# A hybrid encoder layer: the issue order of every engine comes from a list scheduler in the kernel

## The chip, the cores and the metric

The kernel runs on one core of one Trainium2 chip. The metric is device time in microseconds for one execution of the whole layer; three executions are taken and the median counts. Beside them stands one profiled execution, from which every duration in this document comes unless another is named.

## What is computed

One layer of a bidirectional encoder on x of 1024 tokens by 1024 features, all in float32:

```python
x = x + 0.5 * rmsnorm(swiglu(rmsnorm(x), w_gate, w_up, w_down))     # FFN1, 1024 -> 2816 -> 1024
h = rmsnorm(x); z = h @ w_in                                         # 1024 x 3456
y = concat(attention(z[:, :1536]), rwkv7(z[:, 1536:]))
x = x + rmsnorm(y @ w_out)
x = x + 0.5 * rmsnorm(swiglu(rmsnorm(x), ...))                       # FFN2
```

Attention has 8 heads of 64, rotary, with three dilated bands mixed by their softmax denominators. RWKV-7 has 8 heads and runs a delta-rule recurrence over the tokens in both directions:

```python
def _rwkv7_step(state, inp):
    r, w, k, v, kk, kka = inp
    sa = jnp.einsum('dbhvk,dbhk->dbhv', state, kk)
    state = state * w[..., None, :] - sa[..., :, None] * kka[..., None, :] + v[..., :, None] * k[..., None, :]
    y = jnp.einsum('dbhvk,dbhk->dbhv', state, r)
    return state, y
```

## The kernel before

Matrix products are done with each operand split into a rounded high part and a low rest (`split`, L186 on ScalarE and L187 on VectorE) and three matmuls (high x high, high x low, low x high). The stages follow one another in `run`:

- **FFN1**. `_GateUp` multiplies gate and up by a Strassen-like scheme with seven products for each of 22 column blocks j. A product (n, j) is twelve matmuls (L81) into one PSUM tile; `left` loads the weight block and, where needed, builds sums of blocks on VectorE (L60 to L63); `prepare` splits it; `gather` adds the product into rows on VectorE (L86) and applies SiLU on ScalarE (L94). `store` multiplies the halves (L114) and writes seven combinations of the hidden rows to DRAM from GpSimd's queue (L116). `down_sums` builds sums of w_down blocks on GpSimd (L145) and stores them. `down` then loads hidden rows and weight blocks again, splits them (g-tiles) and multiplies (L415).
- **Projection and attention**. `project_attention` and `project_rwkv` (L510) project columns of w_in; the streams r, k, v go to DRAM (`d_rk`, `d_v`, `d_vt`). `attention` runs eight heads through `far` and `near`.
- **Scan**. Tokens are taken in 16 chunks of 64, two to a block, both directions together. For block n, `prep` loads its streams (tile `in`), scales them (L810 to L822), forms products (L830, masked in L832) and stores triangular parts to DRAM; `solve` loads them back as X and inverts by 31 steps of two VectorE operations each (L866, L868), a copy (L870) ends it; `merge` loads the inverses and completes them; `chain` runs the recurrence chunk by chunk, with TensorE (L937, L941, L952), ScalarE (L944, L954, L970) and one state update on VectorE (L968). `prep` and `solve` run up to four blocks ahead of `chain`, in a few buffers. From block 3 on, `project_attended` multiplies attention's rows by their part of w_out in between (L1064, tile `po`), copies the result and stores it (L1084).
- **Finish, projection, FFN2**. `finish_half` normalizes and gates the scan's rows (tiles `f_...`, L995 and on), `out_project` multiplies them (L1064, tile `pw`), adds, normalizes and turns rows, then FFN2 runs as FFN1 does.

The order of work: the program's calls are traced in the order of the Python code. The framework's own scheduler then simulates the engines with its cost model and, for each engine, issues the first call in program order that is ready in the simulation. It also places the tiles in their buffers and sets the waits. In two places the kernel steers it: `high_priority` around the spreading of the first gain row, and `issue_after` around `down_sums`, which ties its GpSimd calls behind the store of the current hidden row. `reuse_waits="tile"` in `pool` makes a tile of a new pool wait only for those old tiles that lay in the same place. DMAs are issued from SyncE (`load`, most stores), GpSimd (`column`, hidden rows, streams, merges) and ScalarE; on each queue they leave in the order of that engine's list, and one that waits holds those behind it. Eight pairs of split weights (`WB`) and eight raw blocks (`RAW`) are buffered.

## Time and profile before

| | us |
|---|---|
| three executions | 2406.85, 2415.44, 2415.84 |
| median | 2415.44 |
| profiled execution, its own time | 2414.54 |
| span of its profile, first to last instruction | 2412.8 |
| HBM traffic, read and written, over the span | 257.53 MB, 125.89 MB |

In the views below, a row of a group gives line, engine, operation, tiles written and read, shape and count; then busy time and the mean of one in ns; then the engine's idle time just before such instructions, and what ended it. A row of a timeline gives the start, the duration and the same names; a q behind the engine's name is its sequencer, which waits and issues DMAs. A row of waits gives the total, the number and the longest. PEclk is the granted TensorE clock, 1.00 being full speed. PE stands for TensorE, DVE for VectorE, ACT for ScalarE, POOL for GpSimd, SP for SyncE. Matmuls are pipelined, so their busy times overlap and their mean is longer than the spacing.

### The profile page before, as it was taken

How to read it: one execution, taken by the hardware profiler on the slowest of the kernel's cores; microseconds unless marked ns; L12 is line 12 of the kernel's file. 1: busy time of each engine (PE TensorE's matmuls, PEld its weight loads, DVE VectorE, ACT ScalarE, POOL GpSimd, SP SyncE). 2: the span in 40 equal slices, each digit the busy share in tenths (PEclk: the TensorE clock that was granted, in tenths of full speed). 3: DMA queues.
4: the chain of work that ended last, by engine and by line, in shares of the span. 5: the costliest groups of instructions: out<-in, count | busy, mean ns of one | idle time of the engine just before them, and what ended most of it. 6: DMA issues, size and time to landing. Idle time of an engine off the chain costs nothing.

```text
span 2412.8 us, 39319 instructions
## 1 busy us (share of the span) xinstructions
PE 2244.5 (93%) x14532; PEld 1817.3 (75%) x14532; DVE 1774.7 (74%) x2949; ACT 1030.6 (43%) x1918; POOL 519.8 (22%) x636
## 2 busy tenths in 40 slices
PE   7999999999999998999987588878979999999997
PEld 5788888788786777787766577764768888887886
DVE  7999999855764446667565887416889999997565
ACT  5333323354675205666444455335542223335453
POOL 2344444300000010111101221103004543442000
PEclk9999999999999998999986597899989999999999
DMA  5344454676644315232376776438644444448655
GB/s 149 127 171 164 154 175 144 217 232 195 200 139 173 122 53 153 82 85 76 92 180 157 165 189 161 116 104 261 224 129 174 170 153 170 155 159 267 192 188 183
DMA packets 359763, 386.03 MB, mean 160 GB/s; under 512 B 73618, under 2 KB 268050, under 8 KB 359572
## 3 DMA queue, kind: packets, MB, share of 16 engines
q1 hardware_dynamic: 314272, 289.02, 39.6%
q0 software_dynamic: 27248, 86.05, 9.6%
q10 hardware_dynamic: 18052, 8.46, 1.3%
q8 instruction: 114, 1.87, 0.3%
q14 instruction: 77, 0.63, 0.1%
HBM read 257.53 MB, written 125.89 MB: 159 GB/s over the span
## 4 chain that ended last, share of the span: by engine, by line
PE 36%; DMA 6%; DVE 4%; ACT 2%; issue 2%; SPq 0%; POOL 0%; DVEq 0%; ACTq 0%; POOLq 0%
PE gu L81 17%; PE pd L415 9%; PE po L1064 2%; DMA in<-d_rk 1%; PE st L937 1%; PE pw L1064 1%; PE y L937 1%; PE lp L830 1%; DMA d_y<-yb 1%; DVE ttmp L866 1%; DVE Ti L868 1%; PE xu L941 1%; PE bp L838 0%; DMA f_y<-d_y 0%; PE pt L330 0%
## 5 line engine op out<-in xcount | busy, mean ns | idle before, releaser
L81 PE MATMUL gu<-xh,wh 128*128 128x512 f32 x704 | 277.9, 395 | 4.1 <-ACT wh L186 3.7
L187 DVE TENSOR_TENSOR wl<-raw,wh 128x512 fp32r<-128x512 f32 (+1 forms) x273 | 275.7, 1013 | 5.0 <-ACT wh L186 4.2
L81 PE MATMUL gu<-xl,wh 128*128 128x512 f32 x704 | 276.7, 393 | 0.0
L81 PE MATMUL gu<-xh,wl 128*128 128x512 f32 x704 | 276.3, 393 | 0.0
L186 ACT ACTIVATE wh<-raw 128x512 fp32r<-128x512 f32 (+1 forms) x273 | 167.8, 627 | 242.6 <-PE gu L81 96.9
L415 PE MATMUL pd<-gl,gwh 128*128 128x512 f32 x616 | 240.5, 390 | 2.5 <-DVE gl L187 2.5
L415 PE MATMUL pd<-gh,gwh 128*128 128x512 f32 x616 | 239.5, 390 | 0.6 <-DVE row L86 0.6
L415 PE MATMUL pd<-gh,gwl 128*128 128x512 f32 x616 | 239.7, 389 | 0.0
L86 DVE TENSOR_TENSOR row<-gu,row 128x512 f32<-128x512 f32 x308 | 206.7, 683 | 22.0 <-PE gu L81 21.0
L187 DVE TENSOR_TENSOR gwl<-graw,gwh 128x512 fp32r<-128x512 f32 (+1 forms) x176 | 118.1, 674 | 129.6 <-ACT gwh L186 127.6
L116 POOL DMA_DIRECT2D d_hid<-row x154 | 85.0, 553 | 562.3 <-DVE row L114 535.9
L186 ACT ACTIVATE gwh<-graw 128x512 fp32r<-128x512 f32 (+1 forms) x176 | 101.4, 576 | 192.7 <-PE pd L415 158.3
L81 PEld LDWEIGHTS gu<-xh,wh 128*128 128x128 f32 x704 | 133.9, 190 | 33.8 <-ACT wh L186 4.7
L81 PEld LDWEIGHTS gu<-xl,wh 128*128 128x128 f32 x704 | 133.7, 190 | 27.7
L81 PEld LDWEIGHTS gu<-xh,wl 128*128 128x128 f32 x704 | 133.5, 190 | 27.9 <-DVE wl L187 0.2
L415 PEld LDWEIGHTS pd<-gl,gwh 128*128 128x128 f32 x616 | 115.6, 188 | 28.1 <-DVE gl L187 4.2
L415 PEld LDWEIGHTS pd<-gh,gwh 128*128 128x128 f32 x616 | 115.5, 188 | 25.2 <-DVE row L86 1.0
L415 PEld LDWEIGHTS pd<-gh,gwl 128*128 128x128 f32 x616 | 115.7, 188 | 23.9
L187 DVE TENSOR_TENSOR gl<-raw,gh 128x512 fp32r<-128x512 f32 x160 | 112.4, 714 | 16.4 <-ACT gh L186 16.1
L94 ACT ACTIVATE row<-row 128x512 f32<-128x512 f32 x44 | 27.8, 632 | 220.5 <-DVE row L86 212.9
L145 POOL TENSOR_TENSOR ws<-ws 128x512 f32<-128x512 f32 x88 | 115.1, 1307 | 1.1
L186 ACT ACTIVATE gh<-raw 128x512 fp32r<-128x512 f32 x160 | 98.0, 621 | 29.2 <-DMA raw<-in_ffn_w_down_dram 21.6
(354 smaller groups left out, 5321.8 us busy)
## 6 DMA issues: line engine op xcount, KB each, us to landing
d_hid<-row POOLq DMA_DIRECT2D x154, 256.0 KB, 2.4
graw<-d_hid SPq DMA_DIRECT2D x132, 256.0 KB, 3.0
raw<-in_ffn_w_gate_dram SPq DMA_DIRECT2D x88, 256.0 KB, 3.1
raw<-in_ffn_w_up_dram SPq DMA_DIRECT2D x88, 256.0 KB, 3.6
ws<-in_ffn_w_down_dram SPq DMA_DIRECT2D x88, 256.0 KB, 4.5
d_ws<-ws POOLq DMA_DIRECT2D x88, 256.0 KB, 2.3
raw<-d_ws SPq DMA_DIRECT2D x88, 256.0 KB, 2.7
raw<-in_ffn_w_down_dram SPq DMA_DIRECT2D x66, 256.0 KB, 3.4
```

Of the source, the lines that this page charges most:

```text
L81: self.K.nc.tensor.matmul(ps, a[:, k, :], b[:, k, :], start=(k == 0 and i == 0), stop=(k == 3 and i == 2))
L86: add = lambda o, x: V.tensor_tensor(o, ps, x, op=OP.add)
L94: A.activation(y[:, 0], y[:, 0], AF.Silu)
L116: put = lambda n, y: G.dma_start(self.hid[n - 1, j // 2], y)
L145: G.tensor_tensor(o, a, b, op=OP.subtract)
L186: self.nc.scalar.activation(h, src, AF.Copy)
L187: (eng or self.nc.vector).tensor_tensor(l, src, h, op=OP.subtract)
L415: T.matmul(ps[x], a[:, ts], b, start=(m == 0 and k == 0), stop=(m == NM - 1 and k == 2))
L830: T.matmul(ps[par][:, pr, :], bk[hs, pr, i, ko:ko + 128], pt[hs, pr, i, :], start=True, stop=True)
L866: V.tensor_tensor(tv, X[:, s, s + 1:][:, :, None].to_broadcast([128, r, m]), Ti[:, s, 0:m][:, None, :].to_broadcast([128, r, m]), op=OP.mult)
L937: add = lambda o, a, b, start, stop: T.matmul(o, a, b, start=start, stop=stop, skip_group_check=True)
L1064: self.nc.tensor.matmul(ps, a[:, k, ts], w, start=(k == 0 and j == 0), stop=(k == 3 and j == 2))
```

## The change

`self.nc` becomes a `_Tape`. Its five engine attributes are recorders: a call such as `nc.vector.tensor_tensor(...)` is noted with its operands and does nothing yet. Pools are wrapped (`_Pool`), so that the tape knows which tile lies in which pool, tag and buffer and where each pool lies in memory. After `run` has recorded everything, `order` computes an order and `play` makes the calls, each tied to the one before it on its engine by an edge that asks for no wait. `wire` finds what each call must come after: calls that touch overlapping parts of a tile or of DRAM, the earlier users of a tile's buffer, and, for a pool that lies where a closed pool lay, all users of that old pool. `cost` gives each call a duration (`took`), a latency to others (`late`), a table-load flag (`load`) and, for a DMA, a time on a wire that all DMAs share (`moved`). `rate` gives each call the length of the longest path from it to the end. `order` walks simulated time: on each engine, among the calls that are ready when the engine is free, the one with the longest path goes first.

The diff, cut to its core (`_Pool` and `mask` only keep accounts of places and of overlapping parts, and are left out):

```diff
+LOADS = {AF.Exp: 1, AF.Sqrt: 2, AF.Silu: 3, AF.Tanh: 4}
...
+    def note(self, eng, method, args, kwargs):
...
+        op.after = [h for h in self.hold if h.eng == eng]
+        self.ops.append(op)
+        return op
+
+    def after(self, op):
+        self.hold = [op] if op else []
...
+    def wire(self):
...
+        for pool in self.pools:
...
+            for q in self.pools:
+                if q.space == pool.space and q.closed is not None and q.closed < pool.opened:
+                    if pool.at < q.at + q.size and q.at < pool.at + pool.size:
+                        q.done = q.done or gate(q.users)
+                        froms[q.done] = 1
+            if froms:
+                g = gate(froms)
+                for op in pool.users:
+                    given[op][g] = 1
+            for _, bufs, tiles in pool.tags.values():
+                for k, name in enumerate(tiles):
+                    if k >= bufs and name in users:
+                        g = gate(dict(users.get(tiles[k - bufs], {})))
...
+    def cost(self, op):
...
+        if op.method == "dma_start":
+            op.took, op.late = (560 if op.eng == "gpsimd" else 360), 1500
+            runs = [math.prod(q[1] for q in a.ap) // (a.ap[-1][1] if a.ap[-1][0] == 1 else 1) for a in (x, *op.ins)]
+            size = math.prod(q[1] for q in x.ap) * 4
+            op.moved = max(size / 320, max(runs) * 1.5)
+        elif op.eng == "tensor":
+            k, m = (op.args[1] if len(op.args) > 1 else x).ap[0][1], x.ap[0][1]
+            if op.method == "transpose":
+                op.took = 112 if k > 64 else 80
+            elif op.args[1].dtype == F32R:
+                op.took = max(64, 0.443 * n)
+            else:
+                op.took = 0.4 * n + 20 if m <= 64 else 0.8 * n + 8
+            op.late = 170
+        elif op.eng == "vector":
+            rate = 1.04
...
+            op.took, op.late = 150 + rate * n + (83 if "accum_out" in op.kwargs else 0), 35
+        elif op.eng == "scalar":
...
+            op.took = 165 + 0.87 * n + 95 * aps + (188 if "accum_out" in op.kwargs else 0)
+            op.load, op.late = LOADS.get(func, 0), 40
+        else:
+            op.took, op.late = (250 + 2.1 * n if op.method != "memset" else 130 + 0.8 * n), 40
+
+    def rate(self):
...
+            op.rank += op.took + op.late + op.moved
+            for p in op.preds:
+                same = p.eng == op.eng and p.method != "dma_start" if p.eng else False
+                p.rank = max(p.rank, op.rank - (p.late if same else 0))
...
+    def order(self):
...
+            t, e = best
+            while later[e] and later[e][0][0] <= t + 1e-6:
+                _, r, n, op = heapq.heappop(later[e])
+                heapq.heappush(heap[e], (r, n, op))
+            _, _, op = heapq.heappop(heap[e])
+            if op.load and op.load != loaded:
+                t, loaded = t + 1283, op.load
+            op.start = t
+            own = free[e] = t + op.took
+            end = own + op.late
+            if op.moved:
+                wire = max(wire, own) + op.moved
+                end = wire + op.late
+            out.append(op)
+            settle(op, end, own)
...
+    def play(self, ops):
+
+        last = {}
+        info = mybir.DependencyInfo(mybir.DependencyClass.NoSync, mybir.DependencyReason.DATA)
+        for op in ops:
+            i = getattr(getattr(self.nc, op.eng), op.method)(*op.args, **op.kwargs).ins
+            if op.eng in last:
+                self.tc.add_manual_dep(i, last[op.eng].name, info, reason="order")
+            last[op.eng] = i
...
-                with self.K.tc.issue_after(self.begun.ins):
-                    self.down_sums(j // 2)
+                self.K.nc.after(self.begun)
+                self.down_sums(j // 2)
+                self.K.nc.after(None)
...
-        self.nc = tc.nc
+        self.nc = _Tape(tc)
...
-        make_identity(nc, self.ident)
+        make_identity(self.tc.nc, self.ident)
...
-                with self.tc.high_priority():
-                    gain = self.spread_row(hand, ring, pt, "ffn1_pre_g")
+                gain = self.spread_row(hand, ring, pt, "ffn1_pre_g")
...
-        _Kernel(tc, io, out).run()
+        k = _Kernel(tc, io, out)
+        k.run()
+        k.nc.play(k.nc.order())
```

More of the change, by code (lines that the diff above doesn't have):

```diff
@@ L1 @@
+import heapq
 import math
@@ L33, in _ap, with __init__, tile, close @@
     return bass.AP(tensor=src.tensor, offset=src.offset + off, ap=pat)
+LOADS = {AF.Exp: 1, AF.Sqrt: 2, AF.Silu: 3, AF.Tanh: 4}
+class _Pool:
+    def __init__(self, tape, real, name, bufs, side, space):
+        self.tape, self.real, self.name, self.bufs, self.side, self.space = tape, real, name, bufs, side, space
+        self.tags, self.opened, self.closed = {}, tape.tick(), None
+        self.stack = tape.stacks.setdefault((space, side), [])
+        self.under = self.stack[-1] if self.stack else None
+        self.stack.append(self)
+        tape.pools.append(self)
+    def tile(self, shape, dtype, name=None, tag=None, bufs=None):
+        tag = tag or name
+        t = self.real.tile(shape, dtype, name=name, tag=tag, **({} if bufs is None else {"bufs": bufs}))
+        g = self.tags.setdefault(tag, [0, bufs or self.bufs, []])
+        size = math.prod(shape[1:]) * 4
+        g[0] = max(g[0], -(-size // 2048) * 2048 if self.space == PSUM else -(-size // 32) * 32)
+        g[2].append(t.tensor.name)
+        self.tape.home[t.tensor.name] = (self, tag, len(g[2]) - 1)
+        return t
+    def close(self):
+        assert self.stack.pop() is self
+        self.closed = self.tape.tick()
+    def place(self):
+        if not hasattr(self, "size"):
+            self.size = sum(size * n for size, n, _ in self.tags.values())
+            base = 0 if self.under is None else self.under.place()[1]
+            self.lo, self.hi = base, base + self.size
+            left, top = self.side == "left", 16384 if self.space == PSUM else self.tape.top
+            self.at = self.lo + (0 if self.space == PSUM else self.tape.base) if left else top - self.hi
+        return self.lo, self.hi
```

171 lines of the change are left out of this document (168 added, 3 removed).

## The prediction

> **What bounds the kernel now.** First the page: the span and the busy engines, then the same by stages, with idle time and TensorE's granted clock beside each other.
>
> ```profile
> span 2412.8 us, 39319 instructions
> ...
> PE 2244.5 (93%) x14532; PEld 1817.3 (75%) x14532; DVE 1774.7 (74%) x2949; ACT 1030.6 (43%) x1918; POOL 519.8 (22%) x636
> ```
>
> ```profile
> core 0: us, PE busy (x) PEld busy (x) DVE busy (x) ACT busy (x) POOL busy (x), PEclk, DMA share, GB/s
> 0.00:80.00 80.00, 61.47 (x262) 46.13 (x263) 63.94 (x106) 42.52 (x78) 12.18 (x24) 0.94 0.45 126
> 80.00:480.00 400.00, 397.98 (x1754) 328.54 (x1753) 382.88 (x418) 123.05 (x215) 179.97 (x209) 1.00 0.50 169
> 480.00:760.00 280.00, 278.35 (x1222) 222.56 (x1221) 181.63 (x265) 169.50 (x297) 3.79 (x7) 1.00 0.57 188
> 760.00:960.00 200.00, 186.90 (x1009) 143.14 (x1008) 87.78 (x162) 64.28 (x119) 14.79 (x21) 0.94 0.37 124
> 960.00:1200.00 240.00, 239.05 (x2201) 191.13 (x2200) 150.65 (x425) 139.12 (x304) 38.02 (x42) 0.97 0.29 83
> 1200.00:1640.00 440.00, 350.65 (x4879) 294.68 (x4877) 269.25 (x756) 192.37 (x356) 70.78 (x108) 0.79 0.60 155
> 1640.00:1800.00 160.00, 132.54 (x584) 97.73 (x584) 129.54 (x205) 81.50 (x158) 19.71 (x16) 0.91 0.62 204
> 1800.00:2160.00 360.00, 360.00 (x1590) 298.05 (x1589) 350.28 (x380) 108.65 (x190) 164.19 (x190) 1.00 0.48 164
> 2160.00:2400.00 240.00, 237.57 (x1044) 195.36 (x1043) 153.58 (x232) 107.79 (x197) 16.40 (x19) 1.00 0.64 207
> ```
>
> Two kinds of stage. In both FFNs (80 to 760 and 1800 to 2400) TensorE is busy 1273.90 of 1280 us at full clock: an order cannot shorten them, only spoil them. The slack is elsewhere: 18.5 us in the start, 13.1 in 760:960, 89.4 in the scan (1200:1640), 27.5 in 1640:1800. In the scan the clock is 0.79 as well, so its 350.65 us of matmuls are not all work at full speed. In attention (960:1200) TensorE has 0.95 us of idle time.
>
> So the scan decides. Which engine does it wait for? VectorE's groups there:
>
> ```profile
> L868 DVE TENSOR_TENSOR Ti<-Ti,ttmp 128x126 f32<-128x126 f32 (+22 forms) x248 | 61.3, 253 | 5.2
> L866 DVE TENSOR_TENSOR ttmp<-X,Ti 128x126 f32<-128x126 f32 (+22 forms) x248 | 61.1, 252 | 9.9 <-DMA X<-d_x 5.0
> L832 DVE TENSOR_TENSOR lm<-lp,k_tri 128x512 f32<-128x512 f32 x64 | 42.9, 686 | 15.9 <-PE lp L830 15.8
> L968 DVE TENSOR_TENSOR sv<-st,gc 64x512 f32<-64x512 f32 x24 | 16.5, 688 | 15.7 <-PE st L937 15.2
> L810 DVE TENSOR_TENSOR pr<-in,e 128x512 f32<-128x512 f32 x16 | 11.0, 689 | 26.2 <-DMA in<-d_rk 25.0 <-PE y L937 1.1
> ...
> L1055 DVE SCALAR_TENSOR_TENSOR wol<-wor,c_attn_out_g,woh 128x512 fp32r<-128x512 f32 x8 | 6.0, 747 | 2.0 <-ACT woh L1054 1.9
> ```
>
> Eight blocks pass through prep and solve on VectorE. Solve (L866, L868) is 122.4 us, prep is L832 with 42.9 and six 128x512 operations of about 11.0 each, of which L810 stands for all: 42.9 + 66.0 = 108.9. That is 231.3 us, 28.9 a block. The first and the last solve end with this copy, and the last chunk of the recurrence with that one:
>
> ```profile
> L870 DVE COPY X<-Ti x8: 587/594/733, 1262.9 to 1548.7; 128x512 f32<-128x512 f32 x8
> ```
>
> ```profile
> L970 ACT COPY yb<-y x32: 352/373/390, 1308.5 to 1618.8; 128x256 f32<-128x256 f32 x32
> ```
>
> From 1262.9 to 1548.7 are 285.8 us, in which VectorE owes seven blocks (7 x 28.9 = 202.3), the state updates (16.5), L1055 (6.0) and the copies of this row (8 x 0.59 = 4.7): 229.5. So up to 56 us of VectorE's time there go into waiting. After the last solve 70.1 us more pass to the last output copy. The end of the scan is this:
>
> ```profile
> 1548.66 0.61 DVE L870 COPY X<-Ti 128x512 f32<-128x512 f32 x1
> 1559.67 1.41 DVE L968 TENSOR_TENSOR sv<-st,gc 64x512 f32<-64x512 f32 x2 [10.40 <-PE st L937]
> ...
> 1575.23 0.68 DVE L968 TENSOR_TENSOR sv<-st,gc 64x512 f32<-64x512 f32 x1 [9.58 <-PE st L937]
> ...
> 1592.40 0.69 DVE L1072 TENSOR_TENSOR yat<-yat,rs 128x512 f32<-128x512 f32 x1 [15.16 <-DMA yat<-d_ya]
> ...
> 1594.35 1.41 DVE L968 TENSOR_TENSOR sv<-st,gc 64x512 f32<-64x512 f32 x2
> ```
>
> A state update every 15.6 us, then 19.1, then 24.5 to the last output copy: 59.1 us for three chunks. In the same stage the SyncE queue holds loads back:
>
> ```profile
> 1602.71 14.43 SPq L1084 DMA_DIRECT2D d_hp<-yao  x4
> 1618.55 0.33 SPq L182 DMA_DIRECT2D g2w<-in_rwkv_g_dram  x1
> 1618.93 1.64 SPq L182 DMA_DIRECT2D f_y<-d_y  x2
> ```
>
> Four stores of the attention half's projection sit ahead of the first loads of the finish stage, each waiting for its copy. The units that finish first need only blocks 2 to 5 of the scan, yet their loads leave after the last block.
>
> **The change part by part.** It adds no arithmetic, tile or DMA; 39319 instructions stay, but for waits and table loads. What moves is the order on five queues, SP's and POOL's DMAs among them, and each term is a wait that a better or worse order changes. Durations are of the profiled execution: 2414.54 us, of which the span is 2412.8; the median of the three runs is 2415.44.
>
> *Scan, middle.* The list takes the ready operation with the longest path behind it. Now prep(1) begins only when solve(0) has ended, and solve(1) 43.7 us after that (a 128x31 step is the first of a solve):
>
> ```profile
> 1262.90 0.59 DVE L870 COPY X<-Ti 128x512 f32<-128x512 f32 x1
> ...
> 1263.48 0.69 DVE L810 TENSOR_TENSOR pr<-in,e 128x512 f32<-128x512 f32 x1
> ...
> 1307.21 0.18 DVE L866 TENSOR_TENSOR ttmp<-X,Ti 128x31 f32<-128x31 f32 x1
> ```
>
> With the longest path first, block 1 goes ahead of blocks 2 and 3, since every later chunk hangs on it, and its loads go out ahead of theirs. Of the 56 us of waiting a part is the latency of store, load and merge between blocks, which no order removes. Ends: 0 and 56; I take somewhat under half, 25.
>
> *Scan, end.* If the state, value and output transfers are issued by landing time, and the projection's long matmuls only where the recurrence waits anyway, a chunk returns to the shorter steps. The shortest seen in these rows is 15.6; the state update itself is 0.69 us, so the rest is a chain of PE, ACT and VectorE that can be shorter when less lies between. Ends: 0, and the whole waiting of VectorE in the rows, 10.40 + 9.58 + 15.16 = 35.1. I take 20, above half, since two of these waits are for L937's matmuls and one for a load, and both stand in queues behind the projection's work.
>
> *Finish stage.* If its first units run beside the last two blocks, what is late next is the second half, which needs the last block. The stage's first wait on TensorE and the row above give the size: 14.43 us of queue, and the wait below of 10.2. Ends 0 and 24.6; I take 15.
>
> ```profile
> PE pt L330 <- DVE xl L187: 14.8, 9, 3.2
> PE lp L830 <- DVE Ti L868: 14.0, 1, 14.0
> ...
> PE yc L995 <- POOL f_y L994: 10.2, 2, 9.2
> ```
>
> *760:960 and 1640:1800.* 13.1 and 27.5 us of idle time, mostly chains of one tile (14.8 us behind L187 is such a chain, in several places). I take a fifth of both, 8; ends 0 and 40.6.
>
> *Start.* 18.5 us idle, waiting for x, then for normalization: same loads, same chain, so I take 0; ends 18.5 to either side, since a load put ahead of x costs what one put behind it gains. Dropping the high priority of the gain row costs nothing: its path to the first product is the longest there is.
>
> *Pool boundaries.* The recorder lets every user of a new pool wait, in its own arithmetic, for every user of the old pool beneath. The program itself waits tile by tile. So loads and splits of a following stage are listed behind the last operations of the previous one, at each FFN's step from gate/up to down first: there a rounding on ACT (below) and its split on VectorE (692 ns, next part), 1.3 us, now hide under matmuls, with the load before them. Two such places and the step into FFN2 at twice that each: minus 8. Ends: 0, and three times as much, as the stages between have such steps too.
>
> ```profile
> L186 ACT ACTIVATE gwh<-graw 128x512 fp32r<-128x512 f32 (+1 forms) x176 | 101.4, 576 | 192.7 <-PE pd L415 158.3
> ```
>
> *FFN interior.* Here VectorE is busy 350.28 of 360 us. Its parts:
>
> ```profile
> L187 DVE TENSOR_TENSOR wl<-raw,wh 128x512 fp32r<-128x512 f32 x114 | 124.4, 1091 | 0.4
> L86 DVE TENSOR_TENSOR row<-gu,row 128x512 f32<-128x512 f32 x135 | 90.5, 682 | 4.5 <-PE gu L81 4.2
> ```
>
> ```profile
> L187 DVE TENSOR_TENSOR gwl<-graw,gwh 128x512 fp32r<-128x512 f32 x54 | 37.4, 692 | 52.7 <-ACT gwh L186 52.6
> ```
>
> The list prices a 512-element VectorE operation at 150 + 1.04 x 512 = 682 ns. That fits L86 and the down stage's split (692), not the gate/up split, 1091 ns, in stages where POOL is busy 46% of the time (164.19 of 360 us; 3.79 of 280 in the down stage). The list thus believes in slack that isn't there. But eight rounded halves are buffered ahead of TensorE and the total work is the same, so I take 0; the price if that cover fails is the rival below. [...]
>
> *ACT tables.* The list charges a table load but does not choose so as to avoid one.
>
> ```profile
> L589 ACT ACT_TABLE_LOAD x4 | 5.1, 1283 | 0.1
> L691 ACT ACT_TABLE_LOAD x4 | 5.1, 1283 | 0.2
> ```
>
> Twice as many of these eight is 10.3 us of ACT, in a stage where ACT is busy 139.12 of 240 us: covered, 0; 10 if the cover is gone.
>
> Sum: 25 + 20 + 15 + 8 + 0 - 8 + 0 = 60 us. 2414.5 - 60 = 2354.5; I say 2354.
>
> **The rivals.** *More is recovered.* The upper ends of the scan and finish terms, 56 + 35.1 + 24.6 = 116, and 8 elsewhere without the boundary cost: 124, so 2414.5 - 124 = 2291. [...] Against: latencies of store, load and merge are inside those waits.
>
> *VectorE starves TensorE in gate/up (slower).* 2 FFNs x 22 column blocks x 7 products = 308 products. TensorE spends 3 x 4 matmuls on each; VectorE has 360 - 350.28 = 9.7 us of slack in 360, or 2.7%. If the order, arranged for splits of 682 ns, makes VectorE wait for TensorE once a product, it cannot make that up. Above 60 / 308 = 0.19 us lost a product the whole change is slower. At the mispricing itself, 0.41 us, it costs 126; at 0.3 us 92, so 2354.5 + 92 = 2447. For it: the two rows above. Against: the eight buffers, and L86 that waits 4.2 us in 135 now.
>
> *Nothing much moves.* The waits are those of the data: solve after load after store, chunk after chunk, two block buffers. Then the scan keeps its end and gains and boundary costs nearly cancel: 8 + 8 - 8 = 8, so 2406. An order that the program doesn't follow would give the same; but each instruction is tied to the one before it on its engine.
>
> **How the numbers follow.** Forecast 0.54, more recovered 0.17, starved 0.16, nothing 0.13. A measurement of this kernel can tell about 0.5%, 12 us, from no change. Faster by more: 0.54 + 0.17 = 0.71; within: 0.13; slower: 0.16. The range runs from 2290, the case that recovers more, to 2430, which takes in no change and mild starvation; left out are most of the starved case (0.11) and what may lie beyond the other (0.07): 0.18. The faster cases alone would be 2290 to 2400.
>
> **What would show it.** Right: scan stage shorter by about 45 us between the first and last L870 and from there to the last L970, solve(1) sooner than 43.7 us after solve(0), f_y loads before the last d_y stores, clock above 0.79, FFN stages with the same length to 5 us. Wrong: L81 waiting for L187 in the FFNs (the starved case); the last L870 as far behind the first as now; the finish loads still behind the recurrence's end.

## The result: slower by 4.5%, and the profile after

| | before | after |
|---|---|---|
| median of four executions (before: the three above and one more), us | 2411.14 | 2516.52 |
| span of the profile, us | 2412.8 | 2515.8 |
| granted clock, mean | 0.944 | 0.929 |

The ratio is 1.0447, 95% interval 1.0406 to 1.0488. The forecast was 2354, the range ended at 2430: wrong in sign. All calls of the new kernel are made from one line of `play` (L335), so its rows are told apart by their tiles. The top of its page:

```profile
span 2515.8 us, 39279 instructions
...
PE 2298.2 (91%) x14532; PEld 1857.3 (74%) x14532; DVE 1637.5 (65%) x2949; ACT 1046.2 (42%) x1918; POOL 537.2 (21%) x636
```

The same number of matmuls takes TensorE 54 us more, while VectorE has 137 us less to show: its work did not shrink, single operations became shorter (below). To see where, both profiles are cut at the same events, not at the same times: end of gate/up, end of down, the first matmul of the r, k, v projection (tile `zr`), the end of attention's last head (`ya`), the first `pr` of prep(0), the last `yb` of the scan, the last output product (`pw`), and the end of the second gate/up. Before:

```profile
core 0: us, PE busy (x) PEld busy (x) DVE busy (x) ACT busy (x) POOL busy (x), PEclk, DMA share, GB/s
0.00:465.90 465.90, 447.05 (x1962) 365.04 (x1963) 435.34 (x510) 160.03 (x284) 185.50 (x225) 0.99 0.48 157
465.90:683.80 217.90, 215.52 (x958) 176.19 (x957) 142.83 (x227) 118.42 (x219) 6.65 (x8) 1.00 0.68 220
683.80:921.50 237.70, 224.27 (x964) 168.72 (x962) 112.36 (x141) 98.86 (x154) 18.58 (x28) 0.97 0.34 122
921.50:1163.20 241.70, 240.11 (x2399) 191.11 (x2399) 163.24 (x480) 148.58 (x334) 30.66 (x30) 0.95 0.30 83
1163.20:1200.20 37.00, 37.00 (x163) 30.63 (x164) 13.13 (x19) 12.57 (x25) 7.36 (x13) 1.00 0.39 124
1200.20:1618.80 418.60, 338.12 (x4828) 285.99 (x4826) 263.94 (x745) 185.94 (x345) 65.70 (x104) 0.79 0.59 150
1618.80:1740.00 121.20, 97.53 (x415) 68.46 (x416) 81.19 (x130) 59.78 (x120) 24.79 (x20) 0.93 0.76 245
1740.00:2186.40 446.40, 433.74 (x1925) 357.67 (x1924) 424.40 (x490) 146.09 (x257) 173.92 (x201) 0.98 0.47 161
```

After:

```profile
0.00:464.50 464.50, 445.38 (x1962) 363.33 (x1963) 355.83 (x506) 165.71 (x285) 194.40 (x225) 1.00 0.48 156
464.50:690.70 226.20, 218.73 (x957) 178.58 (x956) 141.85 (x229) 121.47 (x216) 7.17 (x8) 0.98 0.66 213
690.70:937.70 247.00, 222.21 (x1052) 176.83 (x1050) 117.69 (x154) 101.05 (x164) 18.51 (x28) 0.92 0.34 122
937.70:1240.30 302.60, 293.11 (x2525) 231.22 (x2524) 183.14 (x490) 161.62 (x356) 36.02 (x34) 0.97 0.27 77
1240.30:1257.80 17.50, 16.32 (x81) 13.13 (x82) 5.65 (x8) 6.88 (x14) 4.79 (x10) 1.00 0.83 212
1257.80:1693.90 436.10, 340.35 (x4651) 280.45 (x4650) 262.01 (x738) 172.21 (x325) 64.10 (x102) 0.76 0.53 136
1693.90:1843.70 149.80, 115.71 (x458) 81.17 (x457) 86.72 (x132) 61.87 (x122) 23.75 (x20) 0.82 0.65 209
1843.70:2285.10 441.40, 433.36 (x1931) 357.15 (x1930) 345.16 (x484) 149.42 (x255) 181.63 (x201) 0.99 0.48 158
```

Stage by stage, in us: start with gate/up -1.4, down +8.3, the stage behind it +9.3, attention +60.9, from attention to prep(0) -19.5, scan +17.5, finish and output products +28.6, second gate/up -5.0, and the rest (226.4 against 230.7) +4.3. The sum is 103.0, the difference of the spans.

Three rows carry it. Attention, where TensorE was busy 240.11 of 241.70 us before, got more work and little more waiting (9.5 us of idle time instead of 1.6). What was added is the projection; these are its rows alone, before and after, in attention's window:

```profile
921.50:1163.20 241.70, 80.10 (x239) 43.92 (x239) 11.16 (x18) 0.95 0.30 83
```

```profile
937.70:1240.30 302.60, 134.22 (x438) 79.69 (x438) 21.34 (x36) 0.97 0.27 77
```

The columns are TensorE, its weight load and ScalarE. 199 matmuls, 66 of 176 groups of three, moved from behind attention into it. The scan, from which they went, should then have been shorter. It is longer: TensorE has 95.8 us of idle time in it instead of 80.5, at a clock of 0.76 instead of 0.79. Its marks of before have these counterparts:

```profile
L335 DVE COPY X<-Ti x8: 583/594/766, 1332.6 to 1630.4; 128x512 f32<-128x512 f32 x8
```

```profile
L335 ACT COPY yb<-y x32: 348/372/405, 1361.6 to 1693.9; 128x256 f32<-128x256 f32 x32
```

From the first solve's end to the last are 297.8 us (before 285.8), from there to the last output 63.5 (before 70.1). Where the prediction looked for 25 and 20 us, 12 were lost and 7 gained. Another 12 were lost ahead of both, from the first `pr` to the first solve's end (74.8 us, before 62.7), a stretch for which the prediction had no term.

At first the order did change as forecast. These are the ends of the second, fourth and fifth solve, before and after:

```profile
1345.26 0.59 DVE L870 COPY X<-Ti 128x512 f32<-128x512 f32 x1
1403.60 0.59 DVE L870 COPY X<-Ti 128x512 f32<-128x512 f32 x1
1436.03 0.73 DVE L870 COPY X<-Ti 128x512 f32<-128x512 f32 x1
```

```profile
1353.86 0.60 DVE L335 COPY X<-Ti 128x512 f32<-128x512 f32 x1
1409.58 0.60 DVE L335 COPY X<-Ti 128x512 f32<-128x512 f32 x1
1505.76 0.59 DVE L335 COPY X<-Ti 128x512 f32<-128x512 f32 x1
```

The second solve ends 21 us after the first instead of 82, the fourth 77 instead of 141. Then the fifth comes 96 us behind the fourth instead of 32, and the gain is gone.

### The profile page after: what moved, and what is told of

Read it like the earlier page. It is cut to its first block, busy times and chain, and to the rows that moved or that the text cites. A ratio compares the mean times of both kernels' runs of the same rounds, so it can differ in the third digit from the quotient of the medians.

```text
span 2515.8 us, 39279 instructions
## 1 busy us (share of the span) xinstructions
PE 2298.2 (91%) x14532; PEld 1857.3 (74%) x14532; DVE 1637.5 (65%) x2949; ACT 1046.2 (42%) x1918; POOL 537.2 (21%) x636
## 5 line engine op out<-in xcount | busy, mean ns | idle before, releaser
L335 ACT ACTIVATE wh<-raw 128x512 fp32r<-128x512 f32 (+1 forms) x273 | 167.1, 628 | 396.4 <-PE gu L335 253.6
L335 DVE TENSOR_TENSOR wl<-raw,wh 128x512 fp32r<-128x512 f32 (+1 forms) x273 | 221.5, 821 | 100.8 <-ACT wh L335 59.3
L335 PE MATMUL gu<-xh,wh 128*128 128x512 f32 x704 | 252.3, 393 | 6.7 <-DVE row L335 3.3
L335 DVE TENSOR_TENSOR row<-gu,row 128x512 f32<-128x512 f32 x308 | 204.8, 684 | 80.6 <-ACT wh L335 44.6
L335 PE MATMUL gu<-xl,wh 128*128 128x512 f32 x704 | 251.0, 391 | 0.0
L335 PE MATMUL gu<-xh,wl 128*128 128x512 f32 x704 | 246.1, 390 | 0.0
L335 POOL TENSOR_TENSOR row<-row 128x512 f32<-128x512 f32 x88 | 129.9, 1477 | 520.0 <-DVE row L335 392.7
L335 DVE TENSOR_TENSOR gwl<-graw,gwh 128x512 fp32r<-128x512 f32 (+1 forms) x176 | 110.5, 633 | 137.5 <-PE pd L335 108.3
L335 PE MATMUL pd<-gh,gwh 128*128 128x512 f32 x616 | 180.4, 395 | 13.3 <-DVE row L335 13.2
L335 PE MATMUL pd<-gl,gwh 128*128 128x512 f32 x616 | 180.1, 395 | 0.0
L335 PE MATMUL pd<-gh,gwl 128*128 128x512 f32 x616 | 179.7, 395 | 0.2 <-DVE gwl L335 0.2
L335 ACT ACTIVATE gwh<-graw 128x512 fp32r<-128x512 f32 (+1 forms) x176 | 100.7, 576 | 165.2 <-PE pd L335 139.1
L335 PEld LDWEIGHTS gu<-xh,wh 128*128 128x128 f32 x704 | 132.6, 188 | 38.5 <-DVE row L335 6.7
L335 PEld LDWEIGHTS gu<-xl,wh 128*128 128x128 f32 x704 | 132.6, 188 | 26.9
L335 PEld LDWEIGHTS gu<-xh,wl 128*128 128x128 f32 x704 | 132.0, 188 | 27.3 <-DVE wl L335 0.2
L335 PEld LDWEIGHTS pd<-gh,gwh 128*128 128x128 f32 x616 | 116.4, 190 | 39.0 <-DVE row L335 14.3
L335 PEld LDWEIGHTS pd<-gh,gwl 128*128 128x128 f32 x616 | 116.9, 190 | 25.2 <-DVE gwl L335 0.6
L335 PEld LDWEIGHTS pd<-gl,gwh 128*128 128x128 f32 x616 | 117.1, 190 | 24.8 <-issue 0.2
L335 PE MATMUL lp<-pr,bk 64*128 64x128 f32 x512 | 76.5, 379 | 48.6 <-DVE bk L335 25.6
L335 DVE TENSOR_TENSOR gl<-raw,gh 128x512 fp32r<-128x512 f32 x160 | 115.9, 730 | 6.7 <-ACT gh L335 6.4
L335 ACT ACTIVATE gh<-raw 128x512 fp32r<-128x512 f32 x160 | 99.4, 629 | 47.7 <-PE pd L335 36.7
L335 POOL TENSOR_TENSOR ws<-ws 128x512 f32<-128x512 f32 x88 | 117.7, 1338 | 3.0
```

The lines of the kernel that those rows point to most:

```text
L335: i = getattr(getattr(self.nc, op.eng), op.method)(*op.args, **op.kwargs).ins
```

## The experiments

The medians below are compared with the kernel before on the same chip; ratios are to it. The stages are those of the tables, "scan" always from the first `pr` to the last `yb`. Some expectations cut otherwise: where they give attention 320 us, it is counted from its own first product (in the kernel after from 920.2 to 1240.3), and a scan of 454 us is counted from attention's end. By the tables these two are 302.6 and, with the way to prep(0), 17.5 + 436.1.

### Four single causes

The first theory: the list wrongly took the projection into attention, where TensorE is full, by too low prices or by its ranks; the finish stage suffers from loads that stand behind others on SyncE. The rival: TensorE's work only moves.

**E1, the projection held.**

```diff
+            last = [o for o in nc.ops if o.eng == "tensor"][-1]
...
-            self.project_rwkv(zr, pz, x, [(4, 2), (6, 2), (1, 1), (2, 2)])
+            self.project_rwkv(zr, pz, x, [(4, 2), (6, 2), (1, 1)])
+            nc.after(last)
+            self.project_rwkv(zr, pz, x, [(2, 2)])
+            nc.after(None)
...
+            nc.after(last)
             self.project_rwkv(zr, pz, x, [(8, 2), (10, 2)])
+            nc.after(None)
```

> Edit: the kernel after, with the three blocks of the r, k, v projection that the kernel before computed after attention made to wait for attention's last TensorE operation. Theory A (the projection was moved out of the scan's idle TensorE time into attention, where TensorE is full): attention falls from 320 us to 250 to 270, the scan stays within 10 us of 454 since TensorE stands idle there, and the whole kernel takes 2440 to 2475 us. Rival (TensorE's work is only moved, the sum is conserved): what attention gives back the scan takes, and the time is within 12 us of 2516.

Measured: 2546.54 us, ratio 1.0583 (1.0547 to 1.0618). Attention fell to 263.4 us (by the expectation's cut to 280.9, where 250 to 270 was expected), but the way to prep(0) took 37.7 and the scan 482.7. The theory's first half holds in sign, its second falls: behind attention more was lost than it gave back, 20 and 47 us for 39. The rival, a conserved sum, is nearer, but the time is 30 us above its 2516.

**E2, dearer fp32 matmuls.**

```diff
-                op.took = 112 if k > 64 else 80
+                op.took = 112 if k > 64 else 180
...
-                op.took = 0.4 * n + 20 if m <= 64 else 0.8 * n + 8
+                op.took = max(106, 0.8 * n + 32 if m <= 64 else 1.6 * n + 20) if n < 8 else 0.8 * n + 32 if m <= 64 else 1.6 * n + 20
```

> Edit: the kernel after, with nothing changed but the list's prices of fp32 matmuls, about doubled to what the trace shows (a 64-column transposition 180 ns, small products at least 106 ns). Theory A by its first cause (the list packs too much into attention because it holds attention's own matmuls for cheap): fewer than 110 of the projection's groups of three matmuls stand in attention, against 146, and the time is 2440 to 2480 us. Rival (the order of ranks does it, whatever the prices): 140 or more groups stay there and the time is within 15 us of 2516.

Measured: 2599.12 us, ratio 1.0801 (1.0765 to 1.0837), the slowest of all, and outside both ranges. 145 groups stayed in attention. Too low prices of these matmuls are not why they went there. Nor do the traces show all the new prices: in the kernel after, busy time by count is 116 ns for the two-column products (`kn`, 7.4 us for 64; new price 106), but 96 for the 64-column transpositions (`bp`, 24.5 us for 256; 180) and 52 for the products with the values (`po`, 56.9 us for 1088; 83). The scan took 493.9 us, and its row is worth a look:

```profile
1286.50:1780.40 493.90, 437.11 (x4652) 333.02 (x4650) 264.44 (x738) 173.32 (x326) 64.42 (x102) 0.69 0.47 120
```

TensorE has 57 us of idle time, 39 less than in the kernel after, and as many matmuls take 97 us more, at a granted clock of 0.69.

**E3, program order as rank.**

```diff
-                        heapq.heappush(later[s.eng], (s.ready, -s.rank, s.n, s))
+                        heapq.heappush(later[s.eng], (s.ready, s.n, s.n, s))
...
-                    heapq.heappush(later[op.eng], (0.0, -op.rank, op.n, op))
+                    heapq.heappush(later[op.eng], (0.0, op.n, op.n, op))
```

> Edit: the kernel after, with the operations ranked by their place in the program instead of by the longest path behind them; prices and gates stay. Theory A by its second cause (the ranks put the projection ahead of late attention heads): attention falls to about 250 us and the time to 2420 to 2450 us, about the kernel before. If the prices or the whole-pool gates are at fault, the time stays above 2490 us.

Measured: 2585.15 us, ratio 1.0757 (1.0707 to 1.0806). 119 groups in attention, 277.2 us; scan 542.1. The framework issues by the same rule, first ready in program order, and takes 2407. So ranks explain a part of attention (146 against 119 groups) and none of the total. What is left between the two is whose simulated clock says which call is ready first, the list's, with its prices and its waits for whole pools, or the framework's; most of the 178 us must lie there.

**E4, the output weights by GpSimd.**

```diff
-            W = self.out_weights(self.pool(st, "wo"), 4)
+            W = self.out_weights(self.pool(st, "wo"), 4, queue=nc.gpsimd)
```

> Edit: the kernel after, with the eight loads of the time-mix output weights in the finish stage issued by GpSimd instead of SyncE. Theory C (these loads stand in SyncE's list behind the loads of the finish stage, which wait for the scan's end): the first lands before the finish products begin, the stage from the scan's last output to the last product falls from 150 us to about 130, and the time by 15 to 20 us to about 2498. Rival (the one raw buffer or the VectorE chain sets the stage): the stage stays within 5 us of 150 and the time within 8 us of 2516.

Measured: 2523.17 us, ratio 1.0481 (1.0444 to 1.0517); finish 148.8 us, as the rival had it. The first of these loads now leaves 36.2 us after the scan's last output instead of 43.8, and the stage is no shorter: the queue alone is not the cause.

### The recorder, the list and the binding taken apart

So the change has three parts that can be run alone: calls are recorded and made later, they are made in the list's order, and each is bound to the one before it on its engine. Theory D: the binding costs, since the list's clock is not the chip's. The binding's edges ask for no wait, and in every kernel here, the one before too, each engine's order is fixed when the program is built. "Not bound" means that the framework takes the recorded order as program order and lets its own simulated clock decide which ready call goes first. So what is called the cost of binding here is the order by the list's clock against the same priorities by the framework's.

**E6, not bound.**

```diff
-            if op.eng in last:
-                self.tc.add_manual_dep(i, last[op.eng].name, info, reason="order")
-            last[op.eng] = i
```

> Edit: the kernel after, with the calls made in the list's order but without the edges that tie each to the one before it on its engine, so that the framework's scheduler takes the list's order as program order and issues by its own clock. Theory D (the list's ranks are sound, and what costs is that each engine is bound to an order computed with a clock that the chip does not keep): most of the loss goes, 2410 to 2450 us. Rival R (the list's priorities are bad in themselves, whoever keeps the clock): within 20 us of 2516, or slower.

**E7, the recorder alone**, E6 and:

```diff
-        k.nc.play(k.nc.order())
+        k.nc.play(k.nc.ops)
```

> Edit: the kernel after, with the recorded calls made in the order in which the program made them and no edges: the recorder alone, without the list. If the recorder is neutral, and the framework's own scheduling is what the list replaced: 2400 to 2425 us, the kernel before. Rival (recording itself costs, since pools open and close without calls between and the ties of the weight sums are lost): 2440 us or more.

**E8, the list for the scan alone**, E7 with the part from the projection to the scan's end bound in the list's order; **E9, all but that part**, which is free in program order (E8's order is shown; E9's is its mirror):

```diff
...
-        k.nc.play(k.nc.order())
+        lo, hi = k.nc.part
+        k.nc.play(k.nc.ops[:lo] + [op for op in k.nc.order() if lo <= op.n < hi] + k.nc.ops[hi:])
```

> Edit: as the kernel with the recorder alone, but the operations from the r, k, v projection to the end of the scan are made in the list's order and tied to it; attention, the FFNs and the finish stage are left to the framework. My prediction (the list shortens the scan): 45 us gained, about 2366 us. Rival L (the scan is a loop of latencies through four block buffers, which no order shortens): 2395 to 2430 us. Rival H (the list's order harms the scan by itself, engines standing behind operations that come later than the list believed): 2430 us or more, with a scan from the first prep to the last output of over 430 us against 419 before.

> Edit: the complement: the operations from the r, k, v projection to the end of the scan are left to the framework in program order, all others are made in the list's order and tied to it. If the losses of the kernel after add up by stage: boundaries 7 and finish stage 29 us are kept, attention is no longer than before because the projection is free, so 2411 + 36 = about 2447 us. Rival (attention's own operations are slowed by the list's order even without the projection): attention's heads end 20 us or more after their place in the kernel before, and 2465 us or more.

Measured: E6 2524.86 us (1.0493, 1.044 to 1.0546), E7 2485.84 (1.032, 1.0278 to 1.0361), E8 2571.37 (1.0686, 1.0627 to 1.0746), E9 2454.81 (1.0201, 1.0154 to 1.0248). E7 was a surprise, and its stages say why: both gate/up stages are longer, 506.1 and 483.5 us against 465.9 and 446.4; the scan is 9 us shorter, the others are within 4.

```profile
0.00:506.10 506.10, 456.58 (x1961) 371.33 (x1962) 404.68 (x510) 166.52 (x284) 191.38 (x225) 0.96 0.44 145
1772.90:2256.40 483.50, 444.28 (x1924) 364.82 (x1923) 395.80 (x490) 150.50 (x257) 176.06 (x201) 0.95 0.44 148
```

Without the binding the ties of `down_sums` (`issue_after` before, `hold` after) are lost too, so E6, E7 and E8 carry that loss, and E6's total says nothing on theory D; its scan of 383.7 us does speak for it. E8's scan is 461.4 us, for rival H, and prep(0) begins only 87.0 us after attention's end, before 37.0. E9's attention is 262.6 us with 102 groups in it, finish and products 153.4: its time lies between the sum of the losses and the rival, its attention is the rival's.

**E10 and E11, the same with the ties put back**, in program order and in the list's order:

```diff
-            if op.eng in last:
-                self.tc.add_manual_dep(i, last[op.eng].name, info, reason="order")
-            last[op.eng] = i
+            for h in op.after:
+                self.tc.add_manual_dep(i, last[h].name, info, reason="tie")
+            last[op] = i
```

> Edit: the recorder alone, calls in program order, with the one thing that was lost in that kernel put back: the ties of the weight sums behind the store of the hidden row. If the 78 us that the recorder alone cost lie in those ties (both gate/up stages were 37 to 40 us longer there, all other stages within 5 us of the kernel before): both stages return to 444 to 448 us and the time to 2400 to 2420 us. Rival (something else in recording costs): 2440 us or more.

> Edit: the calls in the list's order with the ties of the weight sums, but not bound on any engine, so that the framework issues by its own clock. Its difference to the kernel after is then the binding alone. Theory D (the binding to the list's clock costs in the scan): the scan from the first prep to the last output is 384 us as in the unbound kernel without ties, against 436, attention stays at 300 to 320, and the time is 2440 to 2465 us. Rival (the unbound scan was short only because the FFNs had shifted everything): scan over 420 us and the time over 2490 us.

**E12**, E10 with only the scan's loop, first merge to last chain, in the list's order (`part` is the loop's first and last call):

```diff
...
-        k.nc.play(k.nc.ops)
+        lo, hi = k.nc.part
+        k.nc.play(k.nc.ops[:lo] + [op for op in k.nc.order() if lo <= op.n < hi] + k.nc.ops[hi:])
```

> Edit: program order with the ties, nothing bound; only the operations of the scan from the first merge to the last chain, the rest of attention's projection among them, are made in the list's order. Theory D with its second half (the list's priorities do shorten the scan, and the gain was paid away in attention): attention 242 us as in the kernel before, scan from the first prep to the last output 380 to 395 against 419, time 2370 to 2390 us, faster than both kernels. Rival L (the scan is a loop of latencies that no priority shortens): 2400 to 2420 us.

**E13**, the kernel after with only that loop not bound, its order kept:

```diff
-            if op.eng in last:
+            if op.eng in last and not self.part[0] <= op.n < self.part[1]:
                 self.tc.add_manual_dep(i, last[op.eng].name, info, reason="order")
-            last[op.eng] = i
+            if not self.part[0] <= op.n < self.part[1]:
+                last[op.eng] = i
...
```

> Edit: the kernel after, all of it in the list's order and bound to it, but for the operations from the first merge of the scan to its last chain, which keep the list's order and lose the binding. Theory D: attention stays at 320 us, the scan from the first prep to the last output falls from 436 to about 385, the time to 2460 to 2475 us. Rival (binding is harmless there): within 12 us of 2516.

| kernel | us | ratio (95%) | attention | scan | finish |
|---|---|---|---|---|---|
| E10 program order | 2418.45 | 1.0044 (1.0023 to 1.0066) | 240.0 | 416.7 | 123.3 |
| E12 list in the loop | 2419.61 | 1.0043 (1.0019 to 1.0067) | 239.3 | 403.5 | 131.3 |
| E11 list, not bound | 2451.01 | 1.0181 (1.0136 to 1.0227) | 303.4 | 393.9 | 143.8 |
| E13 after, loop not bound | 2460.26 | 1.0221 (1.0171 to 1.027) | 305.8 | 383.4 | 148.8 |
| after | 2516.52 | 1.0447 (1.0406 to 1.0488) | 302.6 | 436.1 | 149.8 |

The times of E11 and E13 lie in the ranges of theory D. The binding costs 65 us (E11 to after); lifted in the scan's loop alone it gives 56 back, the scan being 53 shorter (E13). Of these 53, 39 are idle time of TensorE and 14 its busy time:

```profile
1257.20:1640.60 383.40, 326.42 (x4648) 272.70 (x4647) 248.72 (x738) 173.71 (x326) 63.68 (x102) 0.78 0.59 155
```

The list's order by itself costs 33 (E10 to E11; in the two profiles 38): 63 in attention and 20 in the finish stage, against 20 that prep(0) comes closer to attention's end, 23 gained in the scan and smaller ones of both signs elsewhere. E12 misses its 2370 to 2390 us and falls into the range of rival L: the scan gains 13, less than expected, and 8 go back in the finish stage. Even the 13 are not clear of the spread between profiles, since the scan takes 410.0, 404.1 and 407.9 us in E7, E9 and E16 (below), all in program order. In E11, with 23, 178 matmuls fewer stand in the scan than in E10, since the projection went into attention; E12 keeps that as it was. In E12's profile attention also begins 10 us later than in E10, which the edit doesn't touch. So no net gain.

E3 and E10 make the same comparison for program order: the list's clock 2585.15 us, the framework's 2418.45. What is wrong in the list's clock stays open. Dearer matmuls (E2) made it worse; its waits for whole pools and its single wire for all DMAs were not changed.

The scan's parts, with the number of its matmuls; the last column but one is the recurrence itself, from the first `yb` to the last:

| us | first `pr` to first solve's end | to the last solve's end | to the last `yb` | first to last `yb` | matmuls |
|---|---|---|---|---|---|
| before | 62.7 | 285.8 | 70.1 | 310.3 | 4828 |
| after | 74.8 | 297.8 | 63.5 | 332.3 | 4651 |
| E10 program order | 61.4 | 282.6 | 72.7 | 307.9 | 4834 |
| E12 list in the loop | 63.0 | 290.0 | 50.5 | 302.6 | 4782 |
| E11 list, not bound | 76.1 | 264.8 | 53.0 | 288.0 | 4656 |
| E13 after, loop not bound | 74.1 | 256.3 | 53.0 | 277.3 | 4648 |

How one engine's order holds another is seen in the middle of the scan of the kernel after, ahead of the fifth block's solve (its first step is the last row here), in the 96 us that were lost. VectorE:

```profile
1456.41 0.69 DVE L335 SCALAR_TENSOR_TENSOR bk<-bk,th_w 128x512 f32<-128x512 f32 x1
1472.57 0.69 DVE L335 TENSOR_TENSOR th_a<-th_a,in 128x512 f32<-128x512 f32 x1 [15.48 <-ACT th_a L335]
1473.29 1.41 DVE L335 TENSOR_TENSOR sv<-st,gc 64x512 f32<-64x512 f32 x2
1474.73 0.19 DVE L335 TENSOR_TENSOR ttmp<-X,Ti 128x31 f32<-128x31 f32 x1
```

And ScalarE in the same time:

```profile
1465.80 0.58 ACT L335 COPY xs<-xu 128x512 f32<-128x512 f32 x1 [9.69 <-PE xu L335]
1466.28 1.19 ACT L335 ACTIVATE tt<-pb 32x512 f32<-32x512 f32 x2
...
1470.89 1.65 ACT L335 ACTIVATE th_a<-th_a,ka,kah 128x128 f32<-128x128 f32 x4
```

VectorE waits 15.48 us for four short activations of the next prep; they stand in ScalarE's list behind a copy of the recurrence, and this waits 9.69 us for TensorE. The state update and the fifth solve stand behind all of it. TensorE itself is not idle. The first row shows a product taken in one piece; from 1454.4 on three products of the recurrence are taken in turns of one to four matmuls, most of them two:

```profile
1440.93 1.15 PE L335 MATMUL xu<-sv,lm 128*64 128x64 f32 x30
...
1464.64 0.47 PE L335 MATMUL xu<-sv,lm 128*64 128x64 f32 x2
1465.04 0.31 PE L335 MATMUL pb<-tt,d 32*32 32x32 f32 x2
```

```profile
1456.00:1459.00 3.00, 3.00 (x34) 2.34 (x32) 1.09 (x2) 0.10 (x1) 0.00 (x0) 1.00 0.28 90
1459.00:1462.00 3.00, 3.00 (x26) 2.24 (x25) 0.00 (x0) 0.00 (x0) 0.00 (x0) 0.63 0.00 0
1462.00:1465.00 3.00, 3.00 (x22) 2.20 (x22) 0.00 (x0) 0.00 (x0) 0.00 (x0) 0.50 0.00 0
```

In one piece 30 matmuls of `xu` take 1.15 us. In turns 34 matmuls take 3.00 us at full clock, and then the granted clock falls to 0.50. So here the list's order of TensorE makes a delay, and the lists of ScalarE and VectorE pass it on. This is one place; what such places cost in the whole scan was not summed, and the times at which the list's own clock had these calls are not on record. TensorE's waits in the scan, bound and then not (E13):

```profile
PE lp L335 <- DVE bk L335: 25.6, 6, 19.7
PE lp L335 <- DVE gc L335: 12.1, 2, 10.1
```

```profile
PE lp L335 <- DVE bk L335: 8.6, 4, 3.8
```

The longest of them, 19.7 us, lies ahead of the first solve's end, a stretch that is hardly shorter in E13 (74.1 against 74.8 us); the waits of a list do not add up to what it costs.

### Which engine's binding, and the rest

**E14, E15, E19**: the kernel after with one group of engines not bound in the scan's loop, TensorE, SyncE, or VectorE with ScalarE:

```diff
-            if op.eng in last:
+            if op.eng in last and (op.eng != "tensor" or not self.part[0] <= op.n < self.part[1]):
...
```

> Edit: the kernel after with TensorE alone unbound in the scan from the first merge to the last chain; the other four engines stay bound to the list. Which engine's binding costs the 56 us that unbinding all of them there gave back? Theory T (TensorE stands behind products whose operands come late, and a free TensorE would take others): most of it, 2460 to 2480 us, scan from the first prep to the last output 385 to 400 against 436. Rival V (the late operands come from VectorE and ScalarE, themselves bound): under 15 us, 2500 us or more.

> Edit: the kernel after with SyncE alone, which issues most loads and stores, unbound in the scan from the first merge to the last chain. Theory S (the list's landing times put loads and stores behind others that come late): 20 us or more of the 56, below 2497 us. Rival (the DMA order is not what costs): within 12 us of 2516.

> Edit: the kernel after with VectorE and ScalarE unbound in the scan from the first merge to the last chain; TensorE, GpSimd and SyncE stay bound. Rival V of the run with TensorE unbound (the operands of the next block's preparation come late from bound VectorE and ScalarE): most of the 56 us, 2460 to 2480 us. Theory T: under 15 us.

Measured: 2515.53 (1.0435, 1.0394 to 1.0475), 2519.35 (1.0469, 1.043 to 1.0507) and 2508.82 us (1.0411, 1.0368 to 1.0454); scans 430.0, 453.2 and 428.5. By medians none gives back more than 8 of the 56 us, by ratios none more than 9. T, S and V all fall as single causes. That freeing one group does not help while those that it waits for are bound would explain it, but is argued: GpSimd alone, and groups joined across these, were not tried.

**E16, the finish stage alone in the list's order**, E10 elsewhere; the edit of E12 with other ends:

```diff
+            lo = len(nc.ops)
             s_xn, s_fi, s_xr = ExitStack(), ExitStack(), ExitStack()
...
+            nc.parts = [(lo, len(nc.ops))]
             ready(7)
```

> Edit: program order with the ties of the weight sums, nothing bound; only the finish stage and its projection are made in the list's order. In the unbound kernel in the list's order these took 144 us from the last output of the scan to the last product, in program order 123. If the list's priorities do that by themselves: 140 to 146 us and 2432 to 2445 us. Rival (the stage is longer only because the scan before it ends in another way): 121 to 128 us and 2412 to 2424 us.

Measured: 2436.77 us (1.012, 1.0087 to 1.0153), the stage 145.2 us against 123.3. So most of its loss (22 of 28.6 us) comes with the list's priorities, without any binding. The first load of the output weights leaves 45.3 us after the scan's last output, in E10 30.7, in the kernel after 43.8; the products come behind them. E4 shows that sending these loads from another queue is not enough. The clock in the stage is 0.81 (E16) and 0.82 (after) against 0.88 and 0.93 in E10 and before.

**E17, E11 with the hold of E1**, the diffs of both.

> Edit: the unbound kernel in the list's order with the ties (2451 us), and in it the three blocks of the r, k, v projection held behind attention's last TensorE operation, as in the bound kernel with the hold. If attention's length was only the projection put into a full TensorE: attention 303 to 240-250 us, the scan from the first prep to the last output 394 to 400-415, time 2405 to 2425 us. Rival (TensorE's work is only moved, as the bound kernel with the hold showed): within 15 us of 2451 or slower.

Measured: 2468.7 us (1.0256, 1.0221 to 1.029), the rival. Attention 263.1 us, but from the first `pr` to the first solve's end 101.6, where E11 has 76.1 and before has 62.7. The products of prep(0) (`lp`) take from 1248.0 to 1283.8, and the projection's last matmul starts at 1278.3, beside them; before, those products took from 1206.4 to 1223.3, and the projection's last matmul came later, at 1251.4. In E1 as in E17 the list has the held projection done before the products of the one chain that the scan waits for.

**E18, the list only where a run showed a gain**, both gate/up stages and the scan's loop, not bound:

```diff
-        k.nc.play(k.nc.ops)
+        ops, seq, at = k.nc.order(), [], 0
+        for lo, hi in k.nc.parts:
+            seq += k.nc.ops[at:lo] + [op for op in ops if lo <= op.n < hi]
+            at = hi
+        k.nc.play(seq + k.nc.ops[at:])
```

> Edit: program order with the ties, nothing bound, and the list's order only where a run showed a gain: both gate/up stages (unbound in the list's order 439 us against 446 in the second, and a start 8 us sooner) and the scan's loop (13 us shorter). Against the same kernel without these (2418 us) that adds up to minus 28 and plus 8 for the finish stage: 2395 to 2400 us, 0.3 to 0.5% faster than before. Rival (gains of single stages don't add, since the stage behind each pays): 2405 to 2425 us.

Measured: 2408.5 us, ratio 1.0002 (0.9985 to 1.0019): the rival, and the time of the kernel before. The scan is 402.1, the finish stage 129.1, the second gate/up 446.1 us, its gain gone; the first stage (461.1) is quicker than E10's 476.5, whose first product comes 8 us later. No version here beats the kernel before.

## Why the prediction was wrong

- **"Scan, middle" 25 and "Scan, end" 20.** Measured: +17.5 instead of -45. The priorities themselves are worth 13 at most where only the loop has them (E12: the end gains 22, the middle loses 7), and 23 where the projection has left the scan too (E11: the middle gains 18 and the end 20, the stretch ahead of the first solve's end, which had no term, loses 15). What failed above all is the step from a better order in the list's clock to one on the chip: the order as that clock has it costs 42 to 53 us in this stage, makes the middle 12 longer than before and leaves 7 at the end. The prediction named the tie of each instruction to the one before it only as a reason that the order would be kept. It saw that the list prices some work wrongly (the gate/up split, the pool boundaries), but gave the scan no term for a wrong clock.
- The upper end of "Scan, middle" was too low for what it meant: in those 285.80 us VectorE is busy 210.83, so 75 and not 56 wait; the busy times of groups overlap (they add up to 234.7 there) and can't be added. It changes neither the term nor its sign.
- **Attention.** No term. The text noted 0.95 us of idle time in 960:1200 and went on. A stage without slack can't gain, but it can be given work: +60.9, less 19.5 between attention and prep(0). E1 and E17 show that this is not repaired by holding the projection alone.
- **"Finish stage" 15.** Measured +28.6, of which the ranks alone make 22 (E16 to E10). The loads of the scan's rows still leave after its last output, at 1696.6 (last output 1693.9): "late next" was not the second half alone but the weights (E16).
- **"760:960 and 1640:1800" 8.** The first of the two became 9.3 longer, the second lies in the finish stage.
- **Pool boundaries -8.** Down, the stage behind it and the last stage: 8.3 + 9.3 + 4.3 = 21.9 us in all, within the ends given. The cause is open: E11, not bound, has 222.1 and 248.1 us in the first two. Whole-pool waits were not tried by themselves.
- **Start 0, FFN interior 0, ACT tables 0.** Right: -1.4 and -5.0 us, and 18 table loads as before, though the first product starts at 30.2 us instead of 22.0. The starved rival did not come. It named the right place but not the direction: in the second gate/up the split takes 831 ns, before 1019.

```profile
L187 DVE TENSOR_TENSOR wl<-raw,wh 128x512 fp32r<-128x512 f32 x128 | 130.0, 1019 | 0.7 <-ACT wh L186 0.4
L335 DVE TENSOR_TENSOR wl<-raw,wh 128x512 fp32r<-128x512 f32 x128 | 105.3, 831 | 48.7 <-ACT wh L335 29.2 <-PE gu L335 18.7 <-issue 0.8
```

VectorE now waits 48.7 us in the second row, nearly all of it for ScalarE and TensorE, and the stage is 5 us shorter: TensorE was its bound before (busy 433.74 of 446.40 us) and is now (433.36 of 441.40).

- **"Nothing much moves"** had a true half, since the list's priorities alone gained nothing in E12 and E18, but not the price of an order that the list's clock decides. No rival had that as its mechanism, and the one slower rival lay in another stage.

Against the kernel before, the parts are: recorder with ties +11 (E10; its first product starts at 29.6 us, before at 22.0), the list's priorities +33, the binding to the list's clock +65.

## What to carry to other kernels

An order computed ahead is only as good as the simulated clock that made it: here the same priorities cost 65 us more when the list's clock decided than when the framework's did, and for program order the difference was larger still. Run the recorder, the priorities and the clock as three changes. A longest path counts latency but not the queue: here it put long projections ahead of the one short chain that frees the next stage. A stage in which an engine has no idle time belongs in the sum, since a new order can move work into it.

## What the runs showed of the hardware

Less idle time on TensorE did not mean a faster one. In the scan of E2 it stands idle 57 us at a granted clock of 0.69, in that of the kernel after 96 us at 0.76, in E12 53 us at 0.82. Nor does the idle time that the trace shows account for the clock: in the rows above TensorE is shown busy without a pause from 1456 to 1465 us, and the clock falls from 1.00 to 0.50. What lowers it there is open; how far such turns of small matmuls, and not the idle time, make 0.69 of one order and 0.82 of another was not tried.

The length of VectorE's split changes with the order: in the second gate/up it is 1019 ns before and 831 in the kernel after, with GpSimd as busy beside it (173.92 and 181.63 us, 201 operations each). It does not come with the recorder or the binding: in that stage VectorE is busy 424.40 us before and 424.47 in E10, both in program order, 345.16 in the kernel after and 348.29 in E11, both in the list's (490, 490, 484 and 483 operations). What makes the split longer in one order than in the other was not shown.
